# Issuing the 128 spread adaLN weight loads from GpSimd's queue instead of SyncE's

## The chip, the core and the metric

The kernel runs on one core of a Trainium2 chip. The metric is the device time of one execution in microseconds (us), as the median of several runs. A core has five engines that each work through their own queue in order: TensorE (PE, matrix products), VectorE (DVE), ScalarE (ACT), GpSimd (POOL) and SyncE (SP). SP computes nothing here; it only issues transfers (DMAs). An instruction that waits for something holds up everything behind it on its own queue.

## The reference

One layer of a streaming encoder trunk, on x of 512 tokens by 2048 features, all in float32:

```
mod = silu(c) @ w_ada + b_ada                 # 2048 -> 6 * 2048
sh1, sc1, gt1, sh2, sc2, gt2 = split(mod, 6)
h  = rms_norm(x, g_mix) * (1 + sc1) + sh1
xr, yr, q, k, v, f_logit = split(h @ w_in)
y_rec = rglru_group(xr, yr, ...)              # conv, gates, scan, GeLU gate
y_att = forgetting_attention_group(q, k, v, f_logit, ...)   # 8 heads of 128
mix = concat(rms_norm(y_rec), rms_norm(y_att))
x  = x + gt1 * (mix @ w_out)
h2 = rms_norm(x, g_ffn) * (1 + sc2) + sh2
gate, up = split(h2 @ w_up)                   # 2 * 5632 columns
x  = x + gt2 * ((silu(gate) * up) @ w_down)
```

The product with w_ada is a matrix times one vector: 12288 x 2048 weights, 100 MB, each used once.

## The kernel before

**The products.** Each float32 weight tile is split into a high part (ACT, L199, rounded) and a low part (DVE, L200, the difference), and each product is three matmuls: high by high, low by high, high by low (L204). `stream` (L206) loads four row blocks of a weight at a time into one of two `raw` buffers (L210), and splits them in halves into `whi` and `wlo`, three buffers each.

**The stages**, in order of time: the recurrent half of the input projection (w1p, yr0); eight heads of attention, where the products of head h+1 (h1p to h7p) fill PE while the small steps of head h are called from hooks between them; the gate projection (yr1p); the output projection (wo0p to wo3p); the first two column groups of the FFN (up0p, up1p); the rest of the FFN in a fast product of seven parts (uf4p to uf43p); the down projection (dn_0p to dn_3p, twice). The attention score of block b (L515) goes to one of three PSUM buffers of the tag `misc`; DVE reads it (L520, the row minimum nm) and so frees the buffer for the next score but two. Between the halves of the mix, the two RMS factors go DVE (L266), POOL (`rms_rstd`, L250 to L255, then L269), PE (L274), ACT (L277).

**The adaLN product.** A block (j, i) is 128 columns of part j: two tiles of 128 x 1024 float32 (512 KB each), loaded, and multiplied with silu(c) and summed by one DVE instruction for each (L149 or L159). The parts sc1 and sh1 are needed at once and are done by `ada_fast` (L151 to L160). The other four, gt1, sc2, sh2 and gt2, are the spread part: 64 blocks that `queue_ada` puts in a list, and that `ada_some`, called from hooks through the heads, the output projection and the down projection, takes one by one. It runs `ada_block` of one and then calls `ada_load` of the next (L176; not for gt2, whose loads are issued with the block itself). The tiles have the tag `ada` with two buffers, so that the load of a half waits until DVE has done the same half of the block before.

**What sets the order.** The code is not written queue by queue. A scheduling layer puts each instruction on its engine's queue by priorities (`tc.high_priority`, `tc.issue_after`), by the buffers, and by its own estimate of when things will be ready. All transfers of the kernel stand on SP's queue, 905 rows of it. POOL has 42 rows: a few constants at the start, and `rms_rstd` for the heads (`ss`) and for the four RMS factors.

Of the kernel before, what the change touches and what calls it, by code (L numbers as in the profile page):

```python
# [17 lines left out]
KT = D // P  # L18
# [44 lines left out]
def block_kernel(ctx, tc, xT, crow, adaT, vecs, bfr, w1, wyr, wqkv0, wqkv, wgate, wout, wup0, wups, wdown, outT):  # L63
    nc = tc.nc
# [70 lines left out]
    def ada_load(j, i):  # L135
        ts = [ap_.tile([P, 1024], F32, tag="ada", name=f"ada{j}_{i}_{hf}") for hf in range(2)]
        for hf in range(2):
            nc.sync.dma_start(out=ts[hf], in_=adaT[j * KT + i, :, hf * 1024:(hf + 1) * 1024])
        ada_ready[j, i] = ts

    def ada_block(j, i):
        if (j, i) not in ada_ready:
            ada_load(j, i)
        ts = ada_ready.pop((j, i))
        for hf in range(2):
            t = ts[hf]
            cs = c_b[:, hf * 1024:(hf + 1) * 1024]
            ac = ada_acc[j][:, hf, i:i + 1]
            nc.vector.scalar_tensor_tensor(out=t, in0=t, scalar=1.0, in1=cs, op0=ALU.mult, op1=ALU.mult, accum_out=ac)  # L149
# [20 lines left out]
    def ada_some(n, ahead=True):  # L170
        with tc.issue_after(tail_lo[-1]):
            for _ in range(n):
                if pending:
                    pending.pop(0)[1]()
                    if ahead and pending and pending[0][0][0] != GT2:
                        ada_load(*pending[0][0])  # L176
# [946 lines left out]
```

## Time and profile before

| | |
|---|---|
| median of 3 runs | 2127.71 us (2125.3 to 2128.67) |
| the profiled execution, its own time | 2128.95 us |
| its span, first to last instruction | 2127.2 us |
| mean granted clock of TensorE | 0.996 |
| busy, share of the span | PE 98%, DVE 72%, ACT 40%, POOL 2% |
| moved by DMA | 406 MB, 191 GB/s in the mean |
| loads `ada<-in_adaT` issued by line 138 | 128 of 512 KB |

A profile row names its line (L149), engine, operation and tiles as out<-in, with the digits left out: `ada<-in_adaT` is the load of any adaLN tile. "idle before <-releaser" is the time in which an engine stood still just before an instruction, and what ended it. SPq is SP's queue. In a table by stage, each engine's busy time stands with the number of its instructions. A timeline row begins with the start and the duration in us.

### The profile page before, as it was taken

To read this page: it belongs to the slowest core of one execution; us is meant where nothing else is said; L and a number is where in the kernel's file an instruction comes from. 1 tells how busy PE (TensorE), PEld (TensorE's weight loads), DVE (VectorE), ACT (ScalarE), POOL (GpSimd) and SP (SyncE) were. 2 spreads that over 40 slices of the span, in tenths; PEclk is the share of its full clock that TensorE was granted. 3 is DMA by queue.
4 is the path that set the end of the run, shared out by engine and by line. 5 is a ranking of instruction groups with operands and counts; after the bars stand their busy time and mean duration, and the time that the engine had idled before them with its cause. 6 is when DMAs were issued, how large, how long until landed. Compare 5 with 4: busy or idle time off the path is not lost.

```text
span 2127.2 us, 32243 instructions
## 1 busy us (share of the span) xinstructions
PE 2090.5 (98%) x12737; PEld 1898.3 (89%) x12737; DVE 1527.9 (72%) x2403; ACT 858.5 (40%) x1200; POOL 33.9 (2%) x37
## 2 busy tenths in 40 slices
PE   8999999999999998999999999999999999999999
PEld 6889898888788887999999999999999888888887
DVE  8999768886877889888888888888887343323332
ACT  4433447764432346444444444444443222221111
POOL 0000000000100000000000000000000000000000
PEclk9999999999999999999999999999999999999999
DMA  9989766667777622443443443444436984653442
GB/s 336 347 292 318 234 216 218 220 223 260 239 266 260 236 100 99 133 136 125 128 145 120 130 142 126 129 135 130 133 128 199 320 301 171 208 191 134 156 152 100
DMA packets 133016, 406.00 MB, mean 191 GB/s; under 512 B 14561, under 2 KB 19841, under 8 KB 123138
## 3 DMA queue, kind: packets, MB, share of 16 engines
q1 hardware_dynamic: 132866, 403.96, 56.1%
q8 instruction: 99, 1.62, 0.3%
q14 instruction: 51, 0.42, 0.1%
HBM read 361.15 MB, written 42.75 MB: 190 GB/s over the span
## 4 chain that ended last, share of the span: by engine, by line
PE 88%; DVE 7%; DMA 3%; issue 1%; POOL 1%; ACT 1%; SPq 0%; DVEq 0%; ACTq 0%
PE dn_0p L204 6%; PE dn_3p L204 6%; PE dn_2p L204 6%; PE dn_1p L204 6%; PE w1p L204 4%; PE yr1p L204 2%; PE up0p L204 2%; PE wo3p L204 2%; PE wo2p L204 2%; PE wo1p L204 2%; PE up1p L204 2%; PE yr0p L204 2%; PE wo0p L204 2%; PE h3p L204 2%; PE h2p L204 2%; PE h7p L204 2%
## 5 line engine op out<-in xcount | busy, mean ns | idle before, releaser
L149 DVE SCALAR_TENSOR_TENSOR ada<-ada,c_b 128x1024 f32<-128x1024 f32 x128 | 154.6, 1222 | 47.2 <-DMA ada<-in_adaT 46.8
L200 DVE TENSOR_TENSOR uq_0tl<-uq_0r,uq_0th 128x1024 fp32r<-128x1024 f32 x40 | 49.0, 1225 | 62.4 <-ACT uq_0th L199 62.4
L199 ACT ACTIVATE uq_0sh<-uq_0r 128x1024 fp32r<-128x1024 f32 x40 | 42.5, 1062 | 92.6 <-PE uf4p L995 3.8
L200 DVE TENSOR_TENSOR uq_0al<-uq_0r,uq_0ah 128x1024 fp32r<-128x1024 f32 x40 | 49.0, 1225 | 39.7 <-ACT uq_0ah L199 39.6
L199 ACT ACTIVATE uq_1sh<-uq_1rb 128x1024 fp32r<-128x1024 f32 x40 | 42.5, 1063 | 70.7 <-PE uf43p L995 2.4
L199 ACT ACTIVATE uq_0th<-uq_0r 128x1024 fp32r<-128x1024 f32 x40 | 42.4, 1061 | 70.6 <-DVE uq_0r L975 1.9
L199 ACT ACTIVATE uq_1th<-uq_1ra 128x1024 fp32r<-128x1024 f32 x40 | 42.4, 1061 | 68.1 <-PE uf10p L995 1.8
L199 ACT ACTIVATE uq_1ah<-uq_1ra 128x1024 fp32r<-128x1024 f32 x40 | 42.5, 1062 | 60.6 <-issue 59.1
L199 ACT ACTIVATE uq_0ah<-uq_0r 128x1024 fp32r<-128x1024 f32 x40 | 42.4, 1061 | 49.1 <-issue 46.7
L200 DVE TENSOR_TENSOR uq_1tl<-uq_1ra,uq_1th 128x1024 fp32r<-128x1024 f32 x40 | 49.0, 1226 | 10.4 <-ACT uq_1th L199 10.4
L204 PE MATMUL w1p<-hph,w1h 128*128 128x512 f32 x128 | 47.6, 400 | 6.1 <-ACT hph L345 6.1
L200 DVE TENSOR_TENSOR uq_0sl<-uq_0r,uq_0sh 128x1024 fp32r<-128x1024 f32 x40 | 49.1, 1226 | 5.1 <-ACT uq_0sh L199 1.4
L200 DVE TENSOR_TENSOR uq_1sl<-uq_1rb,uq_1sh 128x1024 fp32r<-128x1024 f32 x40 | 49.0, 1226 | 3.7 <-ACT uq_1sh L199 1.5
L204 PE MATMUL w1p<-hpl,w1h 128*128 128x512 f32 x128 | 51.0, 398 | 0.0
L204 PE MATMUL w1p<-hph,w1l 128*128 128x512 f32 x128 | 50.8, 396 | 0.0
L200 DVE TENSOR_TENSOR uq_1al<-uq_1ra,uq_1ah 128x1024 fp32r<-128x1024 f32 x40 | 48.7, 1217 | 0.2
L200 DVE TENSOR_TENSOR dn_1l<-dn_2r,dn_1h 128x1024 fp32r<-128x1024 f32 x11 | 13.5, 1226 | 38.1 <-ACT dn_1h L199 38.1
L159 DVE SCALAR_TENSOR_TENSOR ada<-ada,c_b 128x1024 f32<-128x1024 f32 x32 | 39.1, 1222 | 2.3 <-DMA ada<-in_adaT 2.3
L200 DVE TENSOR_TENSOR dn_0l<-dn_2r,dn_0h 128x1024 fp32r<-128x1024 f32 x11 | 13.5, 1225 | 37.6 <-ACT dn_0h L199 37.6
L200 DVE TENSOR_TENSOR dn_1l<-dn_0r,dn_1h 128x1024 fp32r<-128x1024 f32 x11 | 13.5, 1225 | 37.4 <-ACT dn_1h L199 37.4
L200 DVE TENSOR_TENSOR dn_0l<-dn_3r,dn_0h 128x1024 fp32r<-128x1024 f32 x10 | 12.3, 1225 | 38.0 <-ACT dn_0h L199 38.0
L159 DVE SCALAR_TENSOR_TENSOR adf<-adf,c_b 128x1024 f32<-128x1024 f32 x32 | 39.1, 1222 | 0.1
(13786 smaller groups left out, 8152.5 us busy)
## 6 DMA issues: line engine op xcount, KB each, us to landing
ada<-in_adaT SPq DMA_DIRECT2D x160, 512.0 KB, 5.3
uq_0r<-in_wups SPq DMA_DIRECT2D x80, 512.0 KB, 4.3
uq_1ra<-in_wups SPq DMA_DIRECT2D x40, 512.0 KB, 4.0
uq_1rb<-in_wups SPq DMA_DIRECT2D x40, 512.0 KB, 3.2
adf<-in_adaT SPq DMA_DIRECT2D x32, 512.0 KB, 5.9
actd<-ach SPq DMA_DIRECT2D x44, 256.0 KB, 2.0
actd<-acl SPq DMA_DIRECT2D x44, 256.0 KB, 4.0
dn_0r<-in_wdown SPq DMA_DIRECT2D x11, 1024.0 KB, 4.9
```

Of the source, the lines that this page charges most:

```text
L149: nc.vector.scalar_tensor_tensor(out=t, in0=t, scalar=1.0, in1=cs, op0=ALU.mult, op1=ALU.mult, accum_out=ac)
L159: nc.vector.scalar_tensor_tensor(out=t, in0=t, scalar=1.0, in1=c_b[:, cs], op0=ALU.mult, op1=ALU.mult, accum_out=ada_acc[j][:, hf, i:i + 1])
L199: nc.scalar.activation(R(hi[:, :n]), raw_ap, AF.Copy)
L200: tail_lo.append(nc.vector.tensor_sub(R(lo[:, :n]), raw_ap, hi[:, :n]).ins)
L204: nc.tensor.matmul(ps, lhsT=R(l), rhs=R(r), start=start, stop=stop)
```

## The change

`ada_load` issues its two transfers on GpSimd's queue in place of SyncE's. Data, tiles, sizes and consumers are the same; the loads of `ada_fast` stay on SyncE.

```
     def ada_load(j, i):
         ts = [ap_.tile([P, 1024], F32, tag="ada", name=f"ada{j}_{i}_{hf}") for hf in range(2)]
         for hf in range(2):
-            nc.sync.dma_start(out=ts[hf], in_=adaT[j * KT + i, :, hf * 1024:(hf + 1) * 1024])
+            nc.gpsimd.dma_start(out=ts[hf], in_=adaT[j * KT + i, :, hf * 1024:(hf + 1) * 1024])
         ada_ready[j, i] = ts
```

SP's queue goes from 905 rows to 777, POOL's from 42 to 170. Since the scheduling layer reckons with other times for these loads, some DVE and ACT instructions change places too.

First place: POOL, at the two RMS factors of the mix (`rstd_att` and `ratio`) in the first group of the output projection. `ada3_2_0` is half 0 of block 2 of part 3 (sh2); part 2 is gt1, 4 is sc2, 5 is gt2. Before:

```order
L253 TENSOR_TENSOR ss7_4851<-ss7_4851,mhalf_98 128x8
L250 TENSOR_SCALAR rstd_attt_5317<-rstd_attt_5317 128x4
L252 COPY att_rms_4860<-rstd_attt_5317 128x4
L253 TENSOR_TENSOR rstd_attt_5317<-rstd_attt_5317,mhalf_98 128x4
L255 TENSOR_TENSOR att_rms_4860<-att_rms_4860,rstd_attt_5317 128x4
L250 TENSOR_SCALAR ratiot_5318<-ratiot_5318 128x4
L253 TENSOR_TENSOR ratiot_5318<-ratiot_5318,mhalf_98 128x4
L269 TENSOR_TENSOR ratiot_5318<-ratiot_5318,att_rms_4860 128x4
```

The same place on POOL with the change:

```order
L138 DMA ada3_1_1_5413<-in_adaT 128x1024
L250 TENSOR_SCALAR rstd_attt_5317<-rstd_attt_5317 128x4
L252 COPY att_rms_4860<-rstd_attt_5317 128x4
L253 TENSOR_TENSOR rstd_attt_5317<-rstd_attt_5317,mhalf_98 128x4
L255 TENSOR_TENSOR att_rms_4860<-att_rms_4860,rstd_attt_5317 128x4
L138 DMA ada3_2_0_5526<-in_adaT 128x1024
L250 TENSOR_SCALAR ratiot_5318<-ratiot_5318 128x4
L253 TENSOR_TENSOR ratiot_5318<-ratiot_5318,mhalf_98 128x4
L269 TENSOR_TENSOR ratiot_5318<-ratiot_5318,att_rms_4860 128x4
L138 DMA ada3_2_1_5527<-in_adaT 128x1024
```

One load, `ada3_2_0`, now stands between the two factors, ahead of `ratiot`.

Second place: DVE, at the scores of head 6 (`s6_b` is the score of block b, `nm6_b` its minimum, `sm6_b` its sum, `h73` a weight tile of head 7), where the blocks 8 of part 4 are done. Rows with - stood there before, rows with + stand there now:

```order
 L200 TENSOR_TENSOR h73_0l_4746<-h7r3_4743,h73_0h_4745 128x768
+L149 SCALAR_TENSOR_TENSOR ada4_8_0_4727,ada_acc4_117<-ada4_8_0_4727,c_b_78 128x1024
 L520 ISA bt6_0_4617,nm6_0_4664<-s6_0_4661,bt6_0_4617 128x128
 L520 ISA nm6_0_4664 128x1
 L520 ISA bt6_1_4619,nm6_1_4673<-s6_1_4670,bt6_1_4619 128x256
 L520 ISA nm6_1_4673 128x1
-L149 SCALAR_TENSOR_TENSOR ada4_8_0_4727,ada_acc4_117<-ada4_8_0_4727,c_b_78 128x1024
+L149 SCALAR_TENSOR_TENSOR ada4_8_1_4728,ada_acc4_117<-ada4_8_1_4728,c_b_78 128x1024
 L523 RECIPROCAL sm6_0_4665<-sm6_0_4665 128x1
-L523 RECIPROCAL sm6_1_4674<-sm6_1_4674 128x1
```

The first half of the adaLN block has moved ahead of the first two scores of head 6. Head 2 has the same move: `ada2_4_0` from behind `nm2_0` to ahead of it.

More of the change, by code (lines that the diff above doesn't have):

```diff
@@ L137, in ada_load @@
         for hf in range(2):
-            nc.sync.dma_start(out=ts[hf], in_=adaT[j * KT + i, :, hf * 1024:(hf + 1) * 1024])
+            nc.gpsimd.dma_start(out=ts[hf], in_=adaT[j * KT + i, :, hf * 1024:(hf + 1) * 1024])
         ada_ready[j, i] = ts
```

## The prediction

> **What bounds the kernel now.** I read the page's busy times, then a table by stage, then who waited for whom on PE and on the queue that issues the transfers, and last the timelines at the two places that the order shows. First the page:
>
> ```profile
> span 2127.2 us, 32243 instructions
> PE 2090.5 (98%) x12737; PEld 1898.3 (89%) x12737; DVE 1527.9 (72%) x2403; ACT 858.5 (40%) x1200; POOL 33.9 (2%) x37
> ```
>
> PE is idle for 36.7 us of 2127.2. Anything that the change can win has to come out of that. The table by stage tells where the idle time lies among the stages in which line 138 loads anything (241 to 600 us heads and mix, 600 to 800 output projection and first FFN groups, 1650 to 1850 down projection):
>
> ```profile
> core 0: us, PE busy (x) PEld busy (x) DVE busy (x) ACT busy (x) POOL busy (x), PEclk, DMA share, GB/s
> 241.00:330.00 89.00, 89.00 (x500) 83.58 (x499) 57.50 (x109) 45.25 (x86) 8.34 (x6) 0.98 0.62 201
> 330.00:450.00 120.00, 112.45 (x609) 101.47 (x607) 107.60 (x201) 86.59 (x152) 5.48 (x4) 1.00 0.68 225
> 450.00:550.00 100.00, 99.83 (x503) 86.12 (x504) 71.18 (x128) 52.70 (x95) 5.48 (x4) 1.00 0.71 242
> 550.00:600.00 50.00, 47.72 (x225) 39.08 (x224) 44.76 (x70) 25.33 (x37) 5.77 (x7) 1.00 0.73 245
> 600.00:800.00 200.00, 200.00 (x896) 165.99 (x895) 154.73 (x227) 72.40 (x93) 2.17 (x2) 1.00 0.62 212
> 1650.00:1850.00 200.00, 200.00 (x884) 165.59 (x883) 75.87 (x91) 46.31 (x51) 0.00 (x0) 1.00 0.70 246
> ```
>
> Three stages have none to speak of: 241 to 330, 600 to 800 and 1650 to 1850 are filled, and DVE, which does the adaLN blocks, has room there (57 of 89, 155 of 200, 76 of 200 us). The idle time is 7.55 us in 330 to 450, where DVE itself is busy for 107.6 of 120, and 2.28 us in 550 to 600. So the kernel is bound by PE, and in two short stages by what DVE and the chain of the RMS factors deliver to it. Who ended PE's waits from 241 to 1850 us says the same:
>
> ```profile
> PE s L515 <- DVE nm L520: 3.3, 3, 1.7
> ...
> PE po L542 <- ACT pT L534: 1.9, 1, 1.9
> ...
> PE ratiob L274 <- POOL ratiot L269: 1.5, 1, 1.5
> ...
> PE wo0p L204 <- ACT mx3h L192: 0.8, 1, 0.8
> ```
>
> No wait of PE names a transfer. The loads show up one step earlier, on DVE and on SP's queue (the third row is DVE's own in 330 to 450):
>
> ```profile
> L149 DVE SCALAR_TENSOR_TENSOR ada<-ada,c_b x128: 1198/1221/1237, 264.3 to 1843.1; 128x1024 f32<-128x1024 f32 x128
> ...
>   DMA ada<-in_adaT: 46.8, 29
> ```
> ```profile
> DVE ada L149 <- DMA ada<-in_adaT: 6.2, 5, 1.7
> ```
> ```profile
> SPq L138 <- DVE ada L149: 220.3, 105, 6.6
> ```
> ```profile
> L138 SPq DMA_DIRECT2D ada<-in_adaT x128: 327/328/792, 241.5 to 1817.2; - x128
> ...
> DMA to landing us min/median/max: 3.2/5.2/8.5
> ```
>
> SP's queue stood for 220.3 us, 105 times, until DVE had freed a tile, and then issued in 0.33 us; the load took 3.2 to 8.5 us to land. DVE stood for 46.8 us until loads landed.
>
> **The change part by part.** *Removed:* 128 issues and 220.3 us of standing on SP. What stood behind them there are weight loads and spills; PE never waits for those, so I take this at zero; at most it helps by what a rival below gives. *Added:* 128 issues on POOL, which is 2% busy, so the issuing itself is hidden except where something queues behind it. *Moved:* DVE instructions, as the order shows.
>
> The unknown is g, the time that POOL is taken by one issue: no POOL transfer is in the trace. It lies between SP's 0.33 us and POOL's costliest repeated instruction, 1.71 us; I take 1.10, a POOL instruction at the very place that matters (`ratiot`, below), because it is POOL's own pace while DVE is working.
>
> ```profile
> L253 POOL TENSOR_TENSOR ss<-ss,mhalf 128x8 f32<-128x8 f32 x8 | 13.7, 1712 | 0.7
> ```
>
> The Trainium skill ("DMA: Bandwidth & Descriptors", section "Latency and other measured facts") gives about 1 us to the first byte for a transfer from GpSimd and 0.6 us for one from SyncE: by that each load would land 0.4 us later, not 0.77 (1.10 less 0.33), and the sum below, as an estimate, would come to 2.5 us in place of 2.9. No run so far shows it.
>
> First term, the factor `ratio` of the mix. POOL's timeline, DVE's, SP's and PE's there:
>
> ```profile
> 570.59 1.06 POOL L252 COPY att_rms<-rstd_attt 128x4 f32<-128x4 f32 x1
> 571.73 1.35 POOL L253 TENSOR_TENSOR rstd_attt<-rstd_attt,mhalf 128x4 f32<-128x4 f32 x1
> 573.16 0.26 POOL L255 TENSOR_TENSOR att_rms<-att_rms,rstd_attt 128x4 f32<-128x4 f32 x1
> 573.61 1.10 POOL L250 TENSOR_SCALAR ratiot<-ratiot 128x4 f32<-128x4 f32 x1 [0.19 <-DVE ratiot L266]
> ...
> 575.88 0.31 POOL L269 TENSOR_TENSOR ratiot<-ratiot,att_rms 128x4 f32<-128x4 f32 x1
> ```
> ```profile
> 570.38 1.22 DVE L149 SCALAR_TENSOR_TENSOR ada<-ada,c_b 128x1024 f32<-128x1024 f32 x1
> ...
> 572.14 1.23 DVE L200 TENSOR_TENSOR wo_1l<-wo0r,wo_1h 128x1024 fp32r<-128x1024 f32 x1
> ...
> 573.44 1.22 DVE L149 SCALAR_TENSOR_TENSOR ada<-ada,c_b 128x1024 f32<-128x1024 f32 x1
> ...
> 574.91 1.23 DVE L149 SCALAR_TENSOR_TENSOR ada<-ada,c_b 128x1024 f32<-128x1024 f32 x1 [0.24 <-DMA ada<-in_adaT]
> ...
> 578.07 1.41 DVE L792 SCALAR_TENSOR_TENSOR hsr<-hsr,vec,ratio 128x512 f32<-128x512 f32 x2 [1.93 <-ACT ratio L277]
> ```
> ```profile
> 571.64 0.33 SPq L138 DMA_DIRECT2D ada<-in_adaT  x1
> ```
> ```profile
> 576.25 1.16 PE L274 MATMUL ratiob<-ident,ratiot 128*128 128x128 f32 x8 [1.46 <-POOL ratiot L269]
> ```
>
> L255 ends at 573.42 and `ratiot` starts at 573.61, 0.19 later. The load of `ada3_2_0` now goes in between, so `ratiot` starts g - 0.19 = 0.91 us later, and PE, which stood for it already, stands 0.91 longer (0.14 to 1.52 by the bounds of g). Behind that the same load costs a second time: issued at 571.64 now, it will be issued at 573.42 and out at 574.52, landing 2.9 to 4.9 later (3.2 to 5.2 less SP's 0.33), at 577.4 to 579.4; its DVE block then ends at 578.6 to 580.6, and stands ahead of `hsr`, which could start at 578.07 + 0.91 = 578.98. That is 0 to 1.6 us more for the chain to the mix. Against it, DVE's new order takes `hsr` of the later blocks before an adaLN block of 1.22 us, which can at most remove PE's wait of 0.8 for `mx3h`. I take 0.3 for the two together (-0.8 to +1.6). First term 1.2 us.
>
> Second term, the scores of head 6, on DVE, PE and SP:
>
> ```profile
> 480.13 1.20 DVE L149 SCALAR_TENSOR_TENSOR ada<-ada,c_b 128x1024 f32<-128x1024 f32 x1
> ...
> 483.27 0.28 DVE L520 CUSTOM_DVE_ANT_0 bt<-s,bt 128x128 f32<-128x128 f32 x1
> ...
> 486.75 1.23 DVE L149 SCALAR_TENSOR_TENSOR ada<-ada,c_b 128x1024 f32<-128x1024 f32 x1 [2.78 <-DMA ada<-in_adaT]
> ```
> ```profile
> 486.17 1.07 PE L515 MATMUL s<-qkT,qkT 128*128 128x512 f32 x2
> ```
> ```profile
> 479.11 0.33 SPq L210 DMA_DIRECT2D yr1r<-in_wyr  x1
> ...
> 481.37 0.33 SPq L138 DMA_DIRECT2D ada<-in_adaT  x1
> ```
>
> The half `ada4_8_0` was issued at 481.37, behind a weight load of 1024 KB, and DVE stood 2.78 us for it until 486.75. That cost PE nothing: `nm6_0` had been done at 483.27, ahead of it. Now the block stands ahead of `nm6_0`. Its tile is free when the block of 480.13 ends, at 481.33; with g it is issued by 482.43 and lands 2.9 to 4.9 later, at 485.3 to 487.3. Take 486.3: the block ends at 487.5, `nm6_0` at 487.9 with its 0.28 and the accumulator's read. PE wants to write the fourth score at 486.17, into the PSUM buffer that `nm6_0` frees. It now waits 1.7 us (0.7 to 2.7). What follows in the head moves with PE, so nothing is added.
>
> Head 2 has the same move, and there it should cost nothing, since that load had landed when DVE took the block at 298.80, well after its issue:
>
> ```profile
> 298.80 1.23 DVE L149 SCALAR_TENSOR_TENSOR ada<-ada,c_b 128x1024 f32<-128x1024 f32 x1
> ```
> ```profile
> 301.54 1.07 PE L515 MATMUL s<-qkT,qkT 128*128 128x512 f32 x2
> ```
>
> With 0.77 more the block ends at 300.8 and the minimum 0.4 later, at 301.2, before PE's 301.54.
>
> Third term, the other loads. Each is issued when DVE frees the tile, as before, lands 0.77 us later by g, and earlier by what it no longer queues behind on SP's ring, at most 5.2 - 3.2 = 2.0 us. The two go against each other. Only in 330 to 450 does DVE's time reach PE: five waits there can grow by 3.9 us in all or vanish (6.2 us). I take 0, with -6.2 and +3.9 as ends. In the filled stages a DVE block that is late by a few us is covered by the three buffers of split weights.
>
> Sum: 1.2 + 1.7 + 0 = +2.9 us. On the profiled execution's own 2128.95 us that is 2131.9; that execution lies 1.2 above the median of the three runs, so the forecast for the median is 2127.7 + 2.9 = **2130.6 us**. A difference under 0.2% (4.3 us) can't be told from none with this kernel.
>
> **The rivals.** *The issue on POOL is held by DVE* (slower). Look at the POOL rows above: L252 takes 1.06 us and ends at 571.65, as DVE's block ends at 571.60; `ratiot` takes 1.10 and ends at 574.71, as DVE's next block ends at 574.66; L255 and L269, as small, take 0.26 and 0.31 when no such block runs. So POOL's instructions seem to stand until DVE's two-operand instruction is through. If an issue also stands, for one DVE instruction of 1.22 us beside its own 1.10, g is 2.3. Then the first term is 2.1 + 1.1, the second 2.9, and of the five waits (+2.0 each) I count a third, 3: sum 9, time 2136.8. It decides from g = 1.8, since the first two terms grow by 2 us for each us of g and 4.3 is passed there. Against it: the waits fall only on POOL instructions that read tiles, and an issue may read none. The Trainium skill ("SBUF — State Buffer", section "Who interferes with whom") says that a DVE instruction with two SBUF inputs contends with GpSimd instructions that read SBUF, not with those that only write, and that writing descriptors is blocked by DVE's two-port modes. The trace agrees on the first half, with 1.06 against 0.26 us; by its second half this rival would not come about, and no run so far shows it. Chance 0.28.
>
> *SP's queue is relieved* (faster). Loads no longer queue behind weights and land at the minimum: the waits in 330 to 450 vanish with 6.2 us of PE's 7.55, and the two terms shrink to 0.9 and 0.7. Time 2127.7 - 6.2 + 1.6 = 2123.1. For it: 105 of 128 issues had SP standing. Against it: it stood because no tile was free, and POOL has to wait for the same tile. Chance 0.10.
>
> *All hidden* (no change). An issue on POOL takes SP's 0.33 us, the first term is 0.14, and the load of head 6 overtakes the weights: about 0.5 in all, 2128.2 us. Chance 0.20.
>
> **How the numbers follow.** Forecast 0.42, held by DVE 0.28, relieved 0.10, hidden 0.20. Slower by over 0.2% is the second and a sixth of the first: 0.35. Faster is most of the third: 0.08. The rest, 0.57, is within 0.2%. The range goes from 2124, between the relieved case and the fastest runs of before, to 2138, a little above the held case; that leaves out less than 0.2.
>
> **What would show it.** Right: PE's wait at `ratiob` grows from 1.5 to about 2.4 us; a wait of PE for `nm` of head 6 of 1 to 3 us appears; POOL issues take about 1.1 us; the stages from 600 to 800 and 1650 to 1850 stay filled. Wrong: issues of 2 us or more with waits of DVE for `ada` well above 46.8 us in all, or PE waits in 330 to 450 that shrink from 7.55 us, or any wait of PE in the down projection.

## The result, and the profile after

The changed kernel takes 2150.16 us (median of 4 runs, 2148.69 to 2153.68) against 2128.19 us before (4 runs). The ratio is 1.0106, with a 95% interval of 1.0094 to 1.0118: slower by 22 us. The forecast was 2130.6 us, with 2138 as its upper end, so the time lies far outside. The profiled execution took 2153.68 us, 24.7 more than the profiled one of before; the readings below are made against these two. First the page after, and the table by stage over the same six stretches as in the prediction:

```profile
span 2152.0 us, 32254 instructions
...
PE 2102.0 (98%) x12737; PEld 1905.9 (89%) x12737; DVE 1527.2 (71%) x2403; ACT 856.7 (40%) x1200; POOL 102.7 (5%) x165
```
```profile
core 0: us, PE busy (x) PEld busy (x) DVE busy (x) ACT busy (x) POOL busy (x), PEclk, DMA share, GB/s
...
330.00:450.00 120.00, 114.34 (x605) 103.53 (x605) 106.24 (x198) 86.52 (x152) 18.88 (x29) 0.97 0.65 220
450.00:550.00 100.00, 90.99 (x454) 78.87 (x454) 64.17 (x118) 48.44 (x90) 16.78 (x25) 0.97 0.65 214
550.00:600.00 50.00, 45.95 (x204) 37.38 (x203) 35.80 (x58) 22.10 (x34) 10.57 (x16) 0.93 0.66 227
600.00:800.00 200.00, 195.22 (x853) 160.19 (x853) 147.35 (x211) 65.25 (x84) 18.65 (x33) 0.98 0.66 224
1650.00:1850.00 200.00, 200.00 (x957) 168.79 (x957) 84.06 (x108) 48.29 (x52) 13.28 (x25) 1.00 0.73 263
```

Two columns are to be read. PE is idle for 9.0 us in 450 to 550 (0.2 before), 4.1 in 550 to 600 (2.3) and 4.8 in 600 to 800 (none); the down projection stays filled. And PEclk, which was 1.00 everywhere from 330 to 800, is 0.97, 0.97, 0.93 and 0.98 in these four stretches. PE's *busy* time has grown by 11.5 us too (2102.0 against 2090.5) for the same 12737 matmuls: they ran slower, not only later. Who ended PE's waits from 241 to 1850 us:

```profile
PE s L515 <- DVE nm L520: 7.9, 3, 6.7
PE wo1p L204 <- DVE wo_1l L200: 4.3, 1, 4.3
PE ratioa L265 <- DVE ssq_rec L292: 4.0, 1, 4.0
```

Three single waits: 6.7 us in head 6, 4.0 in the mix, 4.3 in the second group of the output projection. `ratiob`, on which the first term of the sum rested, has no wait any more. This is the clock in the 7 us behind each of the three (same columns as above):

```profile
494.00:501.00 7.00, 5.88 (x16) 4.84 (x17) 6.40 (x21) 3.24 (x9) 1.06 (x2) 0.53 0.54 167
589.00:596.00 7.00, 5.98 (x24) 5.26 (x25) 3.33 (x7) 0.60 (x1) 5.46 (x8) 0.52 0.55 198
654.00:661.00 7.00, 5.68 (x13) 4.46 (x14) 6.49 (x9) 0.00 (x0) 1.06 (x2) 0.51 0.82 272
```

PE is busy for 5.7 to 6.0 of these 7 us, at about half the clock, so some 2.8 us of work are lost at each place: an estimate of 8.4 us for the three. The waits make 15.0, of which before had 1.5 in the mix. 13.5 + 8.4 = 21.9 of the 24.7 us. The page gives the same picture over the whole span: 13.3 us more of idle time (50.0 against 36.7) and 11.5 us more of busy time. The slower work that is left, some 3 us, lies elsewhere, part of it in 330 to 450.

Now the loads themselves (their rows, who waited for them, and the time to landing):

```profile
L138 POOL DMA_DIRECT2D ada<-in_adaT x128: 527/530/742, 174.1 to 1842.2; - x128
...
  DVE ada L149: 72.9, 32
...
DMA to landing us min/median/max: 3.3/5.0/10.5
```

An issue on POOL takes 0.53 us, and POOL has ample time for it. But DVE stood 72.9 us for loads, against 46.8. The median load lands as fast as before (5.0 us against 5.2); the slowest takes 10.5 us against 8.5. So it is a matter of single loads. Head 6, the place that the prediction named, on DVE, PE, POOL and SP:

```profile
493.62 1.23 DVE L149 SCALAR_TENSOR_TENSOR ada<-ada,c_b 128x1024 f32<-128x1024 f32 x1 [8.19 <-DMA ada<-in_adaT]
...
494.77 0.29 DVE L520 CUSTOM_DVE_ANT_0 bt<-s,bt 128x128 f32<-128x128 f32 x1
```
```profile
495.12 2.08 PE L515 MATMUL s<-qkT,qkT 128*128 128x512 f32 x2 [6.71 <-DVE nm L520]
```
```profile
483.82 0.53 POOL L138 DMA_DIRECT2D ada<-in_adaT  x1 [8.39 <-DVE ada L149]
```
```profile
483.26 0.37 SPq L501 DMA_DIRECT2D cb<-cum_d  x1
483.73 3.81 SPq L760 DMA_DIRECT2D hsl<-hsd  x2
```

The mechanism is the forecast one: the block stands ahead of `nm6_0`, and PE waits for `nm6_0`. The size is not: the tile was in place 9.8 us after the start of its issue (483.82 to 493.62), where 2.9 to 4.9 us behind the issue had been taken. And SP, which used to stand until it could issue this load, has gone on: `cb` and both `hsl` are out ahead of it or beside it.

### The profile page after: what moved, and what is told of

Same layout as the page of the kernel before. It is cut to its first block, busy times and chain, and to the rows that moved or that the text cites. A ratio compares the mean times of both kernels' runs of the same rounds, so it can differ in the third digit from the quotient of the medians.

```text
span 2152.0 us, 32254 instructions
## 1 busy us (share of the span) xinstructions
PE 2102.0 (98%) x12737; PEld 1905.9 (89%) x12737; DVE 1527.2 (71%) x2403; ACT 856.7 (40%) x1200; POOL 102.7 (5%) x165
## 4 chain that ended last, share of the span: by engine, by line
PE 78%; issue 8%; DVE 6%; DMA 4%; POOL 2%; ACT 1%; SPq 0%; POOLq 0%; DVEq 0%; ACTq 0%
PE dn_0p L204 6%; PE dn_3p L204 6%; PE dn_2p L204 6%; PE dn_1p L204 6%; PE w1p L204 4%; DMA ada<-in_adaT 3%; PE up0p L204 2%; PE wo3p L204 2%; PE wo2p L204 2%; PE yr0p L204 2%; PE h2p L204 2%; PE h0p L204 1%; PE uf43p L995 1%; PE uf42p L995 1%; PE uf41p L995 1%
## 5 line engine op out<-in xcount | busy, mean ns | idle before, releaser
L149 DVE SCALAR_TENSOR_TENSOR ada<-ada,c_b 128x1024 f32<-128x1024 f32 x128 | 154.5, 1220 | 73.3 <-DMA ada<-in_adaT 72.9
L138 POOL DMA_DIRECT2D ada<-in_adaT x128 | 69.0, 539 | 1512.1 <-DVE uq_1sl L200 852.0
L199 ACT ACTIVATE uq_0ah<-uq_0r 128x1024 fp32r<-128x1024 f32 x40 | 42.4, 1060 | 49.2 <-issue 46.8
L204 PE MATMUL w1p<-hpl,w1h 128*128 128x512 f32 x128 | 50.6, 395 | 0.0
L204 PE MATMUL w1p<-hph,w1l 128*128 128x512 f32 x128 | 50.3, 393 | 0.0
L200 DVE TENSOR_TENSOR dn_1l<-dn_1r,dn_1h 128x1024 fp32r<-128x1024 f32 x11 | 13.5, 1226 | 38.4 <-ACT dn_1h L199 38.4
L200 DVE TENSOR_TENSOR dn_1l<-dn_2r,dn_1h 128x1024 fp32r<-128x1024 f32 x11 | 13.5, 1226 | 37.9 <-ACT dn_1h L199 37.9
L200 DVE TENSOR_TENSOR dn_0l<-dn_2r,dn_0h 128x1024 fp32r<-128x1024 f32 x11 | 13.5, 1225 | 37.6 <-ACT dn_0h L199 37.6
L200 DVE TENSOR_TENSOR dn_0l<-dn_1r,dn_0h 128x1024 fp32r<-128x1024 f32 x11 | 13.5, 1225 | 37.6 <-ACT dn_0h L199 37.6
```

The lines of the kernel that those rows point to most:

```text
L138: nc.gpsimd.dma_start(out=ts[hf], in_=adaT[j * KT + i, :, hf * 1024:(hf + 1) * 1024])
L199: nc.scalar.activation(R(hi[:, :n]), raw_ap, AF.Copy)
L200: tail_lo.append(nc.vector.tensor_sub(R(lo[:, :n]), raw_ap, hi[:, :n]).ins)
L204: nc.tensor.matmul(ps, lhsT=R(l), rhs=R(r), start=start, stop=stop)
```

## The experiments

Two things changed at once, the queue of the loads and the order of the rows on DVE. The theory at this point, **A**: both are needed; a load that lands late costs only where the new order has put its block ahead of a row that PE waits for. Where the text says that an engine keeps an order, every instruction on that engine is tied to the one that went before it in the kernel named, without a wait:

```diff
-    assert not pending
+    hold(tc)
...
+def hold(tc):
...
+        for a, b in zip(names, names[1:]):
+            tc.add_manual_dep(traced[b], a, dep, reason="hold")
```

The places compare best by the time from the first matmul of one tile group to that of the next, since a loss at one place then does not show at the others. The profiled executions give, in us (their own time stands beside the median of the runs):

| kernel | median | profiled | head 7 to yr1 | yr1 to wo0 | wo0 to wo1 | wo1 to wo2 |
|---|---|---|---|---|---|---|
| before | 2128.2 | 2129.0 | 43.5 | 50.8 | 50.3 | 43.5 |
| after | 2150.2 | 2153.7 | 53.1 | 52.7 | 56.0 | 50.8 |
| 1: queue of after, order of before | 2145.3 | 2136.3 | 46.6 | 50.8 | 55.6 | 43.5 |
| 6: the same again | 2145.0 | 2145.0 | 48.9 | 54.7 | 55.2 | 43.5 |
| 2: queue of before, order of after | 2138.0 | 2138.5 | 45.6 | 50.8 | 50.3 | 43.5 |
| 4: ScalarE's queue, order of before | 2157.1 | 2159.6 | 53.6 | 51.1 | 50.8 | 43.5 |
| 7: columns split between SP and POOL | 2134.6 | 2135.2 | 43.6 | 50.8 | 54.8 | 43.5 |
| 9: only GT1 and GT2 on POOL | 2128.8 | 2131.3 | 43.6 | 50.8 | 50.5 | 43.5 |
| 10: 7 with one issue moved on POOL | 2134.0 | 2129.1 | 43.5 | 50.8 | 54.7 | 43.5 |
| 11: ten loads left on SP | 2132.9 | 2137.1 | 43.6 | 50.8 | 50.6 | 44.5 |

The first column of stretches holds scores and weighted sums of head 6, wo0 to wo1 holds the mix. The profiled execution of run 1 is the fastest of its four, 9 us under their median, and shows that much less of the loss. The kernel before ran again beside each run, with medians of 2126.2 to 2128.3 us; the ratios are against those.

**1. The queue alone.** `nc.gpsimd` on line 138 as in the change, DVE, ACT, PE and SP in the order of before.

> GpSimd's queue issues the loads as in the changed kernel, but VectorE, ScalarE, TensorE and SyncE keep the order of the kernel before row for row (SyncE without the loads). Theory A (order and late landing together: a load that lands 7 to 10 us after its issue only costs where the new order of VectorE put its multiply ahead of a row that TensorE waits for, in head 6, in the mix and in the second group of the output projection): nearly all of the 22 us is gone, 2128 to 2134 us, while the longest wait of VectorE for a load may stay at 5 to 8 us. Rival Q (the queue alone: loads on a second queue come too late wherever they stand): 2143 to 2152 us, with the same three places late. Rival S (the relieved SyncE): below 2127 us.

2145.3 us (2136.25 to 2147.18), ratio 1.0088 (1.0072 to 1.0103). Theory A falls: without any move on DVE most of the loss is there, as rival Q had it. But not at the same three places: the output projection's wait is gone. What a load meets in head 6, where DVE, ACT and PE do row for row what they did before (POOL, DVE and SP of this run):

```profile
481.85 0.53 POOL L138 DMA_DIRECT2D ada<-in_adaT  x1 [8.39 <-DVE ada L149]
```
```profile
490.84 1.23 DVE L149 SCALAR_TENSOR_TENSOR ada<-ada,c_b 128x1024 f32<-128x1024 f32 x1 [6.79 <-DMA ada<-in_adaT]
```
```profile
481.28 0.37 SPq L501 DMA_DIRECT2D cb<-cum_d  x1
481.75 3.92 SPq L760 DMA_DIRECT2D hsl<-hsd  x2
```

9.0 us from issue to use; in the kernel before it was 481.37 to 486.75, 5.4 us. The difference on SP: before, `cb` came behind the loads, at 482.94, and one `hsl` only at 488.39:

```profile
481.37 1.48 SPq L138 DMA_DIRECT2D ada<-in_adaT  x2
482.94 0.40 SPq L501 DMA_DIRECT2D cb<-cum_d  x1
...
488.39 0.42 SPq L760 DMA_DIRECT2D hsl<-hsd  x1
```

What the DMA engines did until 486 us, in the kernel before and in this one (from 477):

```profile
DMA packets 648, 2.29 MB, mean 254 GB/s; under 512 B 73, under 2 KB 73, under 8 KB 520
```
```profile
DMA packets 774, 1.84 MB, mean 205 GB/s; under 512 B 56, under 2 KB 361, under 8 KB 646
```

The 256 KB of `cb` come as small packets, and they now run first: 361 packets under 2 KB by 486 us instead of 73, and 0.45 MB less moved. From 484 to 486 us SP's ring has the engines to itself, and no packet of POOL's ring is seen, though its issue was over at 482.38; from 488 to 491 most of the share is POOL's:

```profile
q1 hardware_dynamic: 429, 0.36, 103.2%
...
q0 software_dynamic: 215, 0.79, 64.3%
q1 hardware_dynamic: 183, 0.30, 27.1%
```

The Trainium skill ("DMA: Bandwidth & Descriptors", section "Queues, rings and completion order") says that a DMA engine goes round the queues that have work, packet by packet. By that POOL's packets should have had a share as soon as they stood in their ring, and these rows do not show when that was. In run 7 below, POOL's first packets are seen at 488.0 us, 2.2 us after the end of the issue; here at 486.4 us, 4.0 us after it. So for nearly 2 us the share was missing here, or the packets reached their ring that much later; which of the two is not shown.

That gives theory **F**: the load lost its place. As long as SP issued it, everything that stood behind it on SP went out later; now these transfers go ahead of it. Its rival **R**: packets of a second queue come late whenever SP's is busy, whoever issued first.

**2. The order alone.** `nc.sync` as before, DVE, ACT, PE and SP in the order of after.

> SyncE issues the loads as in the kernel before, but VectorE, ScalarE and TensorE keep the order of the changed kernel row for row, and SyncE that order too with the loads put in. Theory A: the loads land in 3 to 6 us as in the kernel before, so the multiplies that stand ahead cost 0 to 3 us in all: 2127 to 2132 us up to the down projection's start (head 7's first matmul late by under 3 us, up0's by under 4). Rival O (the order alone): 2140 to 2152 us, up0's first matmul late by 15 us or more. In the down projection a few of the loads now stand on SyncE ahead of weight pieces, which may cost some us of its own after 1640 us; that is read apart.

2138.0 us (2136.02 to 2140.11), ratio 1.0051 (1.0038 to 1.0063). PE's waits in head 6, and at the start of the down projection:

```profile
PE s L515 <- DVE nm L520: 1.8, 1, 1.8
...
PE dn_0p L204 <- DVE dn_0l L200: 6.0, 1, 6.0
```

Up to the down projection the order costs 1.9 us (the first matmul of wo0 and of up0 come 1.9 later than before); head 6 alone has 2.1 (45.6 against 43.5). Rival O falls. The other 8 us appear between the first two groups of the down projection, where this kernel, unlike the other two, has three loads of GT2 on SP ahead of a weight piece; they say nothing of the change.

**3 and 7. The place on SP's queue given back.** SP loads a small part of each tile where it used to load the whole, and so stops there as before; GpSimd loads the rest. Run 3, against line 138 of run 1:

```diff
+nc.sync.dma_start(out=ts[hf][:16], in_=adaT[j * KT + i, :16, ...])
-nc.gpsimd.dma_start(out=ts[hf], in_=adaT[j * KT + i, :, ...])
+nc.gpsimd.dma_start(out=ts[hf][16:], in_=adaT[j * KT + i, 16:, ...])
```

> As the run with GpSimd's queue and the order of before, but SyncE loads the first 16 of the 128 partitions of every ada tile itself, at the place and with the wait for the buffer that the whole load had in the kernel before; GpSimd loads the other 112. So 7/8 of the bytes still go through GpSimd's queue, but SyncE again stops at each of these places, and what stands behind them (the carry tile cb and hsl in head 6) starts as late as before. Theory F (the load is late because the relieved SyncE issues later transfers ahead of it, cb with its 512-byte packets first): the tile of head 6 is in place 5 to 6.5 us after its issue, and the median is 2128 to 2134 us. Rival R (packets of a second queue are served late whenever SyncE's queue is busy, whoever issued first): 8 us and more in head 6, and 2136 to 2147 us, as with the whole load from GpSimd.

2162.7 us, ratio 1.0161 (1.0135 to 1.0187), and it decides nothing: GpSimd's part waited for SP's part to land, and was issued that much later. Among the rows of the tile on who waited for it:

```profile
  POOL ada L138: 123.6, 26
```

Run 7 splits by columns (0 to 127 and 128 to 1023), where no such wait arises.

> The third run again, mended: there GpSimd's part of each tile waited until SyncE's part had landed. Now SyncE loads columns 0 to 127 of each ada tile, at the place and with the buffer's wait of the kernel before, and GpSimd columns 128 to 1023, which waits for the buffer alone; all else in the order of before. Theory F (the relieved SyncE issues later transfers, cb above all, ahead of the load): the tile of head 6 is in place 5 to 6.5 us after GpSimd's issue, 2128 to 2136 us. Rival R (a second queue's packets come late whenever SyncE's queue is busy, whoever issued first): 8 us or more in head 6, and 2136 to 2150 us.

2134.6 us (2130.05 to 2136.43), ratio 1.0028 (1.0015 to 1.0041). Head 6 on POOL, DVE and SP:

```profile
485.29 0.54 POOL L138 DMA_DIRECT2D ada<-in_adaT  x1 [8.38 <-DVE ada L149]
```
```profile
490.47 1.22 DVE L149 SCALAR_TENSOR_TENSOR ada<-ada,c_b 128x1024 f32<-128x1024 f32 x1 [2.98 <-DMA ada<-in_adaT]
```
```profile
484.92 1.48 SPq L138 DMA_DIRECT2D ada<-in_adaT  x2
486.44 0.46 SPq L501 DMA_DIRECT2D cb<-cum_d  x1
```

7/8 of the bytes still come through POOL's queue, `cb` stands behind again, and the tile is in use 5.2 us after its issue, as in the kernel before (5.4). Head 6 costs nothing (43.6). F is right there and R falls. Of the queue's loss of 17.6 us (run 1) 6.2 are left, each against the kernel before beside it. The mix has kept 4.5 us. Everything behind the loads on SP got its old place back at once, so the run does not tell `cb` from `hsl`.

**4. Another second queue.** `nc.scalar` on line 138, otherwise as run 1.

> The order of the kernel before on VectorE, TensorE, SyncE and among ScalarE's computing, with the 128 loads issued from ScalarE's queue (a hardware queue of its own) in place of GpSimd's. Theory F and any rival by which a second queue is the trouble: the load of head 6 takes 7.5 us and more from issue to landing, and SyncE's cb is again ahead of it; 2134 us or more. Rival S (it is the software queue of GpSimd that is slow beside other traffic): 5 to 6 us there, 2126 to 2132 us. ScalarE may also stand still behind an issue that waits for its buffer, which both would show as waits on ScalarE and is read apart.

2157.1 us, ratio 1.0131 (1.0115 to 1.0148). ScalarE's queue and DVE in head 6:

```profile
505.80 1.48 ACTq L138 DMA_DIRECT2D ada<-in_adaT  x2
```
```profile
515.41 1.23 DVE L149 SCALAR_TENSOR_TENSOR ada<-ada,c_b 128x1024 f32<-128x1024 f32 x1 [7.07 <-DMA ada<-in_adaT]
```

9.6 us, with SP's `cb` at 505.08 again just ahead. So in head 6 it isn't that GpSimd's queue is a software one: rival S falls. The total says little, since ScalarE itself was held up in heads 4 to 6 (its share cannot be separated here).

**5 and 8. The clock by itself.** Into the kernel before, in the up projection, where PE, past its first group, otherwise never waits: ahead of some groups PE must wait for a chain on VectorE and GpSimd.

```diff
+LADDER = {10: 0, 14: 1, 18: 2, 22: 3, 26: 4, 30: 6, 34: 8, 38: 12}
...
+                nc.vector.tensor_copy(out=lad, in_=last_m[3][:, :8])
+            for _ in range(LADDER[f]):
+                nc.gpsimd.tensor_scalar_add(lad, lad, 1.0)
+            step = nc.tensor.matmul(ps[0][:, :8], lhsT=ones, rhs=lad, start=True, stop=True)
```

> The kernel before with eight waits built into the up projection, where TensorE otherwise has none: ahead of groups 10, 14, 18, 22, 26, 30, 34 and 38 TensorE must wait for a chain of one copy on VectorE and 0, 1, 2, 3, 4, 6, 8 and 12 small additions on GpSimd behind the last matmul of the group before. Theory G (the clock): a wait under about 3 us costs its own length, a wait of 4 us or more costs its length and 3 to 4 us more, because the granted clock is 0.50 for some 7 us behind it, as behind the three long waits of the changed kernel (6.7, 4.3 and 4.0 us). Rival H (the low clock there had another cause, such as the load of the DMA engines): every wait costs its own length, the clock stays 1.00, and the sum is the sum of the waits.

One execution, 2201.0 us. The eight waits came out at 4.2 to 9.0 us. The groups behind them took 1.5, 2.5, 2.4, 2.2, 1.8, 2.7, 2.9 and 2.3 us longer than their 20.2, the next group nothing. Rival H falls: a wait by itself lowers the clock behind it. Theory G is right in kind and too high in size, since it had 3 to 4 us. Run 8 starts the chain from an earlier product of the group before, for shorter waits.

> As the ladder of eight waits, but with shorter ones: the chain starts from a product that TensorE ended earlier, so ahead of groups 8, 12, 16, 20, 24, 28, 32, 36 and 40 the waits should come out between 0.5 and 4 us. Theory G: groups behind waits under about 3 us take their usual 20.2 us, those behind waits of 3.5 us and more take 1.5 to 3 us longer; in between either may be seen.

One execution, 2191.0 us. They came out at 3.1 to 5.7 us, so the ladders leave the part under 3 us untried. Three of the nine, and below them, in order of time (groups 8, 20, 24), the clock in the 7 us behind each:

```profile
PE uf8p L997 <- DVE lad L994: 4.9, 1, 4.9
...
PE uf24p L997 <- POOL lad L996: 3.5, 1, 3.5
PE uf20p L997 <- DVE lad L994: 3.1, 1, 3.1
```
```profile
922.00:929.00 7.00, 6.54 (x33) 6.55 (x34) 1.78 (x4) 1.72 (x3) 0.00 (x0) 0.55 0.48 186
...
1187.00:1194.00 7.00, 6.96 (x45) 6.96 (x46) 4.13 (x8) 2.95 (x4) 0.00 (x0) 0.76 0.66 225
1273.00:1280.00 7.00, 6.86 (x45) 6.86 (x46) 3.73 (x8) 2.95 (x4) 0.08 (x1) 0.76 0.66 224
```

The waits of 3.1 and 3.5 us cost 1.5 and 1.4 us behind them, those of 4.9 us 2.4 and 2.6. All 17 waits of the two ladders cost something.

Below 3 us there are only the waits that the kernels have anyway. Two stretches of the kernel before: 7 us behind the wait of PE that ended at 226.09 (2.9 us, for `nm`), and 7 us with no wait of PE anywhere in 241 to 330:

```profile
226.00:233.00 7.00, 6.91 (x29) 5.93 (x30) 5.82 (x21) 5.45 (x18) 0.00 (x0) 0.76 0.72 251
280.00:287.00 7.00, 7.00 (x35) 7.00 (x36) 4.78 (x9) 2.96 (x5) 1.86 (x1) 0.76 0.77 241
```

So 2.9 us sufficed here, and in run 11 a wait of 2.9 us (for `wo_1l`, below) did not: the clock stayed at 1.00 in the 7 us behind it. And the clock also falls where PE has not waited; why stays open.

**6. Run 1 again**, for a profile nearer its median.

> The kernel of the first run again, for a profile of an execution at its median (2145 us; the one profiled took 2136). Theory G: where the 9 us more come from are one to three waits of TensorE that were 2.0 to 2.4 us there and are over 3 us here, each with 3 to 4 us of a clock of 0.50 behind it, in heads 6 to 7 or in the mix. Rival: a lower clock all along, or losses spread over many places.

2145.0 us, one execution. Head 6 and the stretch yr1 to wo0 each have more than in run 1 (48.9 and 54.7): a wait of 3.0 us in head 6 with a clock of 0.83 over 500 to 510 us, and 1.9 us of idle PE in 540 to 550 with 0.83 as well. In run 1 the wait at the same place in head 6 was 2.4 us, and the clock stayed at 1.00. So the spread of this kernel's runs is in part the clock: a wait a little longer or shorter can decide whether it is lowered. The 0.50 over 7 us that theory G expected was not seen there.

**9. Half of the loads.** `(nc.gpsimd if j in (GT1, GT2) else nc.sync)` on line 138, order of before on all engines.

> Only the loads of GT1 (heads 2 to 4) and of GT2 (down projection), 64 of the 128, go through GpSimd's queue; those of SC2 and SH2 stay with SyncE, and all engines keep the order of the kernel before. Theory A: no row that TensorE waits for comes late there, so 2126 to 2130 us, the same as before. Rival (any load on a second queue costs, or the relieved SyncE gains): over 2132 us, or under 2125 us.

2128.8 us, ratio 1.0008 (0.9999 to 1.0017): the same. These 64 loads are followed by no row that PE is about to wait for, and cost nothing on GpSimd's queue; neither does relieving SP of them gain anything.

**10. The mix.** In runs 1 and 7, GpSimd issued the load `ada3_2_0` behind the chain of the attention half's RMS factor and, by then, behind SP's 1 MB piece of wo1. Here the issue (block 2 of SH2, first half) comes two steps earlier.

```diff
@@ the order on GpSimd @@
 L252 COPY att_rms<-rstd_attt 128x4
+L138 DMA ada_2_0_5594<-in_adaT 128x896
 L253 TENSOR_TENSOR rstd_attt<-rstd_attt,mhalf 128x4
 L255 TENSOR_TENSOR att_rms<-att_rms,rstd_attt 128x4
-L138 DMA ada_2_0_5594<-in_adaT 128x896
```

> The column split again, with one instruction moved: the issue of the load ada3_2_0 stands on GpSimd between the second and the third step of the mix's sum for the attention half (COPY att_rms and TENSOR_TENSOR rstd_attt), where its buffer has just come free, and no longer behind the whole chain, some 2.1 us later and behind SyncE's 1 MB piece wo1r. Theory P (in the mix the loss is GpSimd's own order: the load waited behind the chain and so fell behind wo1r): the first matmul of wo1 comes 50 to 51.5 us behind that of wo0 (54.8 in the column split, 50.3 in the kernel before), and the median is 2129 to 2132 us. Rival (the loss in the mix comes from the second queue as such, wherever the issue stands): still 53 us or more, and 2133 to 2137 us.

2134.0 us (2129.13 to 2137.22), ratio 1.0041 (1.0027 to 1.0056), and 54.7 us in the mix: theory P's numbers are missed. Its wait did go. The block that waits for this load on DVE, and the stretch of PE behind:

```profile
573.87 1.23 DVE L149 SCALAR_TENSOR_TENSOR ada<-ada,c_b 128x1024 f32<-128x1024 f32 x1 [0.85 <-DVE ada L149]
```
```profile
574.00:581.00 7.00, 6.19 (x20) 4.96 (x19) 4.15 (x7) 2.30 (x4) 2.24 (x4) 0.51 0.74 271
```

DVE no longer stands for the load (4.79 us in run 1). But the issue now lies inside the chain, PE waits three times in short order around it, 0.88, 0.98 and 0.81 us, and the clock falls to 0.51. In runs 1 and 7 it had stayed at 1.00 through the mix (558 to 598 us), with single waits of up to 2.0 us. So the mix loses as much as in run 7, by another way; that the three waits are what lowered the clock is argued from their place, not tested.

**11. Ten loads on SP.** `(nc.sync if (j, i) in ON_SP else nc.gpsimd)`, with blocks 8 and 9 of SC2 and 1, 2 and 3 of SH2 in `ON_SP`; order of before.

> 118 of the 128 loads go through GpSimd's queue; ten stay with SyncE: those of blocks 8 and 9 of SC2 (head 6) and of blocks 1, 2 and 3 of SH2 (the mix). All engines keep the order of the kernel before. Theory L (the cost of the queue lies in these few loads, each of which stands ahead of a row that TensorE is about to wait for): heads 6 to yr1 43.5 to 44.5 us and wo0 to wo1 50.3 to 51 us, as in the kernel before, and 2127 to 2132 us. Rival (the cost is spread over all loads of SC2 and SH2, or comes from a second busy queue as such): 2135 us or more, with one of the two places still late by 2 us or more.

2132.9 us (2129.98 to 2137.06), ratio 1.0028 (1.0015 to 1.0041): a little over theory L's upper end. Both places are as in the kernel before (43.6 and 50.6), so of the queue's 17.6 us 6.6 are left (against 2126.3 for the kernel before beside it), and these ten loads carry 11. Of what is left, most turned up elsewhere in the profiled execution, the slowest of the six, in the third group of the output projection (DVE had stood 3.2 us for a load ahead of this `wo_1l`):

```profile
PE wo2p L204 <- DVE wo_1l L200: 2.9, 1, 2.9
```

So L holds for the two places and not for the whole: the other loads of SH2 cost now and then. A version faster than the kernel before was not found, and nothing in these runs points to one.

## Why the prediction was wrong, point by point

- **"What stood behind them there are weight loads and spills; PE never waits for those, so I take this at zero."** This is the step that failed. Behind the loads on SP stood `cb` and `hsl` too, and the 220 us of standing held them back. Relieved of it, SP sent them ahead of the loads. Shown for head 6 by run 7 against run 1: the same queue, order and almost the same bytes, 5.2 instead of 9.0 us until the tile is used, and 10.7 us less in all. Head 6 makes 9.6 of the 24.7 us (53.1 against 43.5); the mix and the second group of the output projection come below, and are not all of this step.
- **Second term, 1.7 us in head 6.** Place and chain of waits were right, and with loads from SP's queue in the new order the wait is 1.8 us (run 2). Its size hung on a landing of 2.9 to 4.9 us behind the issue, taken from the least to the median time to landing in the kernel before; the same row had 8.5 as its longest. Here it was over 9.
- **A wait costs its length.** Nowhere stated, used in every term. Behind each of the three long waits PE ran at about half clock for some 7 us, an estimate of 8.4 of the 24.7 us. The stages of the table that have waits could not show it: with waits of at most 1.9 us in 330 to 800 PEclk was 1.00 there. But the profile before has a wait of 2.9 us at 226.09, with a clock of 0.76 over the 7 us behind it, which is 1.7 us of work. The Trainium skill ("TensorE: Matmul & The Clock Gate", section "HAM oscillation — how this bites in real kernels") says that gaps of PE over about 3.4 us throw it back to half clock. The ladders agree in kind, but 3.1 us already sufficed there, and 2.9 us in the kernel before.
- **"In the filled stages a DVE block that is late by a few us is covered by the three buffers of split weights."** Wrong in the output projection of after: two blocks that waited for loads stood ahead of the split `wo_1l`, and PE waited 4.3 us. With the order of before that wait is gone, and with SP's queue too (43.5 us from wo1 to wo2 in runs 1 and 2): in these profiled executions both changes were needed there, as theory A said. The order is not always needed: run 11 has a like wait, 2.9 us for `wo_1l` one group later, in the order of before.
- **First term, the mix, 1.2 us.** `ratiob` does not wait any more, since the chain ahead of it came late: PE waits 4.0 us for `ssq_rec` first. DVE was behind there; from 535 to 562 us it had stood 8.1 us for three loads (2.1 for two in the same stretch before), and then 2.7 us for ACT, which waited for a spill (`yal`) to come back. That this is the cause is read from the rows, not tested. The second price of the same load, DVE standing for it ahead of `hsr`, was named with 0 to 1.6 us, and was 4.8 in run 1. That SH2's loads from SP cure the mix is shown (run 11). In runs 1 and 7 the clock stayed at 1.00 there, so their loss is waiting. How much of it is the late issue and how much the transfer ahead stays open: run 10 removed DVE's stand for the load, and the total stayed, this time with a lower clock.
- **g = 1.10 us, and the rival that DVE holds the issue.** It measured 0.53, at most 0.74. The rival came out nearest in time, for a reason that did not exist.
- **The down projection loses nothing, and SP's relief gains nothing at PE.** Right for the loads of GT1 and GT2; run 9 shows both at once.

## What to carry to other kernels

A DMA issue that waits for a buffer is also a gate for everything behind it on its queue. Before moving it to another queue, look at what stands behind it, and ask where that will go: small-packet transfers that come free may run ahead of the load that was moved. And price a wait of TensorE over some 3 us at its length and 1.4 to 3.2 us more, for the clock (the ladders, and the three places of the changed kernel); from 2 to some 3 us these traces show both a lowered clock and none.

## What the runs showed of the hardware

- An issue on GpSimd took 0.53 us, at most 0.74: none was held for the length of a DVE row (1.22 us).
- Behind the 17 waits of the ladders (3.1 to 9.0 us) the granted clock was 0.53 to 0.76 over 7 us, and the loss 1.4 to 2.9 us. It does not follow the length of the wait: 2.5 us behind 4.6 us, 1.8 behind 6.1.
- Behind a wait of 2.9 us the clock was 0.76 over 7 us in the kernel before, and 1.00 in run 11. Behind three waits of 0.8 to 1.0 us within 6 us it was 0.51 in run 10, and without any wait 0.76 over 280 to 287 us in the kernel before; the cause of these two is open.
- The fastest load lands as fast from one queue as from the other (least time to landing 3.2 us on SP before, 3.3 us on GpSimd after). In head 6 a load from GpSimd's or ScalarE's queue came into use 9.0 to 9.8 us after its issue when `cb`, a transfer of small packets, had been issued less than 1 us ahead on SP's; with `cb` issued behind it, 5.2 us (run 7).
